# Starting every large on-chip tile at a multiple of 256 bytes in a hybrid decoder block

## The chip, the core and the metric

The kernel runs on one core of a Trainium2 chip. The metric is device time in microseconds (us) of one execution, the median of several runs. The profile is one execution recorded by the hardware profiler; its span runs from the first to the last instruction.

## The reference

The reference is one decoder layer in fp32 over 512 tokens of width 2048. It normalises the tokens, projects them with one large matrix, and splits the columns in two groups: four heads of gated linear attention and four of differential softmax attention. Both outputs go through one output projection and are added to the residual. Then follows a gated MLP with a short causal convolution.

```python
def token_mixer(h, ...):
    proj = h @ w_in                                   # (512, 2048) @ (2048, 6160)
    gq, gk, gv, gg, ga, dq, dk, dv = split(proj)
    o_a = gla_chunked(gq, gk, gv, log_sigmoid(ga @ w_alpha_up + b_alpha) / 16)
    o_a = rmsnorm(o_a, gla_norm) * silu(gg)
    o_b = rmsnorm(diff_attention(dq, dk, dv, lam), diff_norm) * (1 - lambda_init)
    return concatenate([o_a, o_b]) @ w_o              # (512, 2048) @ (2048, 2048)

def conv_ffn(h, ...):
    a, b = split(h @ w_ffn_in)                        # (512, 2048) @ (2048, 2 x 5632)
    a = conv_w[0] * a[t-2] + conv_w[1] * a[t-1] + conv_w[2] * a[t] + conv_b
    return (gelu(a) * b) @ w_ffn_out                  # (512, 5632) @ (5632, 2048)

x = x + rmsnorm(token_mixer(rmsnorm(x, attn_pre_norm)), attn_post_norm)
x = x + rmsnorm(conv_ffn(rmsnorm(x, ffn_pre_norm)), ffn_post_norm)
```

## The kernel before

**Precision.** Large products are made of three fp32r matmuls. Each operand is split into a high part (`act(hi, raw, AF.Copy)` on ScalarE, L110) and the rest (`tt(lo, raw, hi, subtract)` on VectorE, L111). TensorE then adds high x high, high x low and low x high in PSUM. The normalised activations lie in `ah` and `al` (high and low, each `[128, 4, 16, 128]`: partition, block of 128 tokens, block of 128 features, token or feature). The weights come through `raw` or `rt` (as loaded, 4096 bytes per partition) and are split into `whi` and `wlo`, or `xhi` and `xlo` where a fourth buffer is to be had. The small products inside the two kinds of attention, and the transposes against `ident`, are plain fp32.

**Stages, in order of time.** First the head: load the tokens, normalise and transpose them into `ah`/`al`. Then the projections of the mixer, and the output projection:
- `proj_t` and `mm_t` (L146 to L148) stream `ah`/`al` as the moving operand, 512 columns in four pieces of 512 bytes, 8192 bytes apart, against weights from `whi`/`wlo`. The last few stream 256 columns, in two pieces.
- `proj_n` and `mm_n` (L164 to L166) do it the other way round: `whi`/`wlo` move, 2048 contiguous bytes, and a 128-token block of `ah`/`al` is the stationary operand.

The attention heads are generators that run between these projections (`step`, `fill`). Their plain fp32 matmuls include L481 (scores) and L512 (values); L131 is a transpose.

The up-projection of the MLP (827 to 1690 us) uses a Strassen-like scheme with seven products in place of eight. `up_prods` (L893 to L895) streams 256 columns in two pieces of 512 bytes. For four of the seven products they are blocks of `ah`/`al`, with the pieces 8192 bytes apart. For the other three they are sums in tiles of their own, `s5h`, `s5l`, `s2h`, `s2l`, `s3h`, `s3l`, with the pieces 4096 bytes apart. The weights of these products are loaded by SyncE's queue, and partly added to by transfers that GpSimd issues (L842).

The down-projection (1690 to 2105 us) has the same scheme in `down_prods` (L990 to L992), where `whi`/`wlo` or `xhi`/`xlo` move with 512 columns. `last_group` (L1097 to L1099) adds the first columns of the MLP and writes the result.

**Where tiles lie.** Each pool takes its place in the on-chip memory in the order in which the pools are made, from the low end unless `side="right"` is given; every tile is rounded up to 32 bytes per partition. The low 16,384 bytes are not the kernel's, then come four constants of 32 bytes each. Before the change `ident` (512 bytes) and `nhalf` (32) follow, so `ah` begins at 17,056, and everything behind it inherits an odd offset, with small tiles of 32 bytes between. Per partition, in bytes from the start of the memory:

```text
tile             before               after
ah               17056 (160 mod 256)  16640 (0)
al               49824 (160)          49408 (0)
raw              85728 (224)          82176 (0)
whi              102112 (224)         98560 (0)
wlo              114400 (224)         110848 (0)
rt               126688 (224)         123136 (0)
s5h, s2h, s3h    143072, ... (224)    139520, ... (0)
xhi, xlo (MLP)   192352, ... (96)     188672, ... (0)
ident            16512 (128)          225536 (0)
```

All offsets in the column "before" are multiples of 32 and not of 64, except that of `ident`.

Of the kernel before, what the change touches and what calls it, by code (L numbers as in the profile page):

```python
# [9 lines left out]
F32 = mybir.dt.float32  # L10
# [7 lines left out]
P = 128  # L18
D = 2048
S = 512  # L20
NT = S // P
# [6 lines left out]
NF = DFF // P  # L28
# [7 lines left out]
def hybrid_layer(ctx: ExitStack, tc: tile.TileContext, x, attn_pre_norm, w_in, w_alpha_up, b_alpha,  # L36
# [3 lines left out]
    nc = tc.nc  # L40
# [6 lines left out]
    def dma(o, i):  # L47
        return nc.sync.dma_start(out=o, in_=i)
# [7 lines left out]
    mm = nc.tensor.matmul  # L56

    const = ctx.enter_context(tc.tile_pool(name="const", bufs=1))
    small = ctx.enter_context(tc.tile_pool(name="small", bufs=8))
    psm = ctx.enter_context(tc.tile_pool(name="psm", bufs=4, space=PSUM))  # L60
    psa = ctx.enter_context(tc.tile_pool(name="psa", bufs=4, space=PSUM))

    wpool = ctx.enter_context(tc.tile_pool(name="w", bufs=3))

    ident = const.tile([P, P], F32, name="ident")
    make_identity(nc, ident)
    nhalf = const.tile([P, 4], F32, name="nhalf")
    nc.vector.memset(nhalf, -0.5)

    ah = const.tile([P, NT, KT, P], F32R, name="ah")  # L70
    al = const.tile([P, NT, KT, P], F32R, name="al")

    def bank(pool=None):
        return (pool or psa).tile([P, 512], F32, name="bank", tag="bank")
# [21 lines left out]
    def load(src, a):  # L96
        raw = wpool.tile([P, GR], F32, name="raw", tag="raw", bufs=4)
        dma(raw.rearrange("p (a b) -> p a b", a=a), src)
        return raw

    def granule(src, a, raw=None, spare=None, bufs=4):
        if raw is None:
            raw = load(src, a)
        if spare:
            hi = spare.tile([P, GR], F32R, name="xhi", tag="xhi", bufs=bufs)
            lo = spare.tile([P, GR], F32R, name="xlo", tag="xlo", bufs=bufs)
        else:
            hi = wpool.tile([P, GR], F32R, name="whi", tag="whi")
            lo = wpool.tile([P, GR], F32R, name="wlo", tag="wlo")
        act(hi, raw, AF.Copy)  # L110
        tt(lo, raw, hi.bitcast(F32), ALU.subtract)  # L111
        r = "p (a b) -> p a b"
        return hi.rearrange(r, a=a), lo.rearrange(r, a=a)

    def rsqrt_mean(ss, n, width=1):
        t = small.tile([P, width], F32, name="ms", tag="ms")
        nc.gpsimd.tensor_scalar(t, ss, 1.0 / n, EPS, ALU.mult, ALU.add)
        r = small.tile([P, width], F32, name="rs", tag="rs")
        nc.gpsimd.tensor_tensor(r, t, nhalf[:, :width], ALU.pow)
        return r  # L120
# [5 lines left out]
    def transpose_into_act(src, t, slot0, n):  # L126
        for g in range(0, n, 4):
            m = min(4, n - g)
            b = bank()
            for j in range(m):  # L130
                nc.tensor.transpose(b[:, j * P:(j + 1) * P], src[:, (g + j) * P:(g + j + 1) * P], ident)  # L131
            bv = b[:, :m * P].rearrange("p (k c) -> p k c", k=m)
            split(ah[:, t, slot0 + g:slot0 + g + m, :], al[:, t, slot0 + g:slot0 + g + m, :], bv)

    def bcast_row(tile_ap, row):
        dma(tile_ap, row.partition_broadcast(P))
# [23 lines left out]
    def mm_n(banks, t, g, w):  # L160
        for k in range(2):
            s = 2 * g + k
            st, sp = s == 0, s == KT - 1
            mm(banks[t], ah[:, t, s, :], w[0][:, k, :], start=st, stop=False)  # L164
            mm(banks[t], ah[:, t, s, :], w[1][:, k, :], start=False, stop=False)  # L165
            mm(banks[t], al[:, t, s, :], w[0][:, k, :], start=False, stop=sp)  # L166
# [17 lines left out]
    def big8(name):  # L184
        return mx.tile([P, 2048], F32, name=name, tag="big8", bufs=6)
# [8 lines left out]
    def first_half(c):  # L194
        gb = big8("gb")
        jb = mx.tile([P, 1024], F32, name="jb", tag="jb", bufs=1)
        xts = [big8("xt") for _ in range(NT)]
        H2 = [slice(1024 * i, 1024 * (i + 1)) for i in range(2)]
        H4 = [slice(512 * i, 512 * (i + 1)) for i in range(4)]
        rs, raws, w = {}, {}, {}  # L200
        banks = [bank(psm) for _ in range(NT)]
        col = C_GV + 512 * c

        def load_x(t):
            for i in range(2):
                dma(xts[t][:, H2[i]], x2[t * P:(t + 1) * P, H2[i]])

        def load_w(*gs):
            for g in gs:
                raws[g] = load(w_in3[:, 2 * g:2 * g + 2, col:col + 512], 2)  # L210

        def weights(g):
            w[g] = granule(None, 2, raws[g], spare=mx if g == 3 else None, bufs=1)

        def square(t):
            ss = small.tile([P, 2], F32, name="ss2", tag="ss2")
            for i in range(2):
                act(jb, xts[t][:, H2[i]], AF.Square, accum_out=ss[:, i:i + 1])
            sm = small.tile([P, 1], F32, name="ss", tag="ss")
            nc.gpsimd.tensor_tensor(sm, ss[:, 0:1], ss[:, 1:2], ALU.add)  # L220
            rs[t] = rsqrt_mean(sm, D)

        def scale(t, *ps):
            for i in ps:
                stt(xts[t][:, H4[i]], xts[t][:, H4[i]], rs[t], gb[:, H4[i]], ALU.mult, ALU.mult)

        def turn(t, *ps):
            for i in ps:
                transpose_into_act(xts[t][:, H4[i]], t, 4 * i, 4)

        def prods(t, *gs):
            for g in gs:
                mm_n(banks, t, g, w[g])

        load_x(0)
        bcast_row(gb[:, H2[0]], attn_pre_norm[0, H2[0]])
        load_w(0, 1, 2)
        load_x(1)
        load_w(3)
        load_x(2)  # L240
        load_x(3)
        bcast_row(gb[:, H2[1]], attn_pre_norm[0, H2[1]])
        square(0)
        scale(0, 0, 1)
        weights(0)
        turn(0, 0, 1)
        weights(1)
        weights(2)
        square(1)
        prods(0, 0, 1)  # L250
        scale(1, 0, 1)
        prods(0, 2)
        weights(3)
        turn(1, 0, 1)
        square(2)
        prods(0, 3)
        square(3)
        scale(2, 0, 1)
        prods(1, 0, 1, 2)
        turn(2, 0, 1)  # L260
        prods(1, 3)
        scale(3, 0, 1)
        prods(2, 0, 1)
        turn(3, 0, 1)
        scale(0, 2, 3)
        prods(2, 2)
        turn(0, 2, 3)
        scale(1, 2, 3)
        prods(2, 3)
        turn(1, 2, 3)  # L270
        scale(2, 2, 3)
        prods(3, 0, 1)
        turn(2, 2, 3)
        scale(3, 2, 3)
        prods(3, 2)
        turn(3, 2, 3)
        prods(3, 3)
        return banks
# [30 lines left out]
    bcast_row(dnb, diff_norm[0])  # L309
    ts(dnb, dnb, 1.0 - LAMBDA_INIT, None, ALU.mult)  # L310

    lam = const.tile([P, 1], F32, name="lam")
    lt = setup[:, 0:512].rearrange("p (a d) -> p a d", a=4)
    for i, v in enumerate((lambda_q1, lambda_k1, lambda_q2, lambda_k2)):
        bcast_row(lt[:, i, :], v[0])
# [7 lines left out]
    tt(lam, le[:, 0:1], le[:, 1:2], ALU.subtract)  # L323
    ts(lam, lam, LAMBDA_INIT, None, ALU.add)

    cols = const.tile([P, 4 + 4 * NF], F32, name="cols")
    rows = setup[:NF, 1536:2048].rearrange("p (a d) -> p a d", a=4)
    ba = setup[:4, 768:896]
    dma(ba, b_alpha[0].rearrange("(h d) -> h d", d=P))
# [266 lines left out]
    wp = wo.enter_context(tc.tile_pool(name="wo", bufs=1))  # L596
# [2 lines left out]
    g2 = wp.tile([P, D], F32, name="g2")  # L599
    bcast_row(g1, attn_post_norm[0])  # L600
    bcast_row(g2, ffn_pre_norm[0])
    ssm = [wp.tile([P, 4], F32, name=f"ssm{t}") for t in range(NT)]

    def evac_m(c, t, b):
        jk = wp.tile([P, 512], F32, name="jk5", tag="jk5", bufs=1)
# [218 lines left out]
    ff = None  # L824
# [224 lines left out]
    ff = ctx.enter_context(tc.tile_pool(name="ff", bufs=2))  # L1049
    acc = [ff.tile([P, D], F32, name=f"acc{t}", bufs=1) for t in range(NT)]  # L1050
    accp = [ff.tile([P, D // 2], F32, name=f"accp{j}", bufs=1) for j in range(2)]
    ssf = [ff.tile([P, 4], F32, name=f"ssf{t}", bufs=1) for t in range(NT)]
    g3 = ff.tile([P, D], F32, name="g3", bufs=1)
    bcast_row(g3, ffn_post_norm[0])
    downs[0].z0()
# [135 lines left out]
```

## Time and profile before

| | |
|---|---|
| Median of 3 runs | 2177.14 us (2175.53 to 2177.21) |
| The profiled execution's own time | 2177.07 us |
| Its span | 2175.4 us |
| TensorE busy | 2140.5 us (98%) |
| VectorE, ScalarE, GpSimd busy | 65%, 41%, 9% |
| Moved by DMA | 303.83 MB, mean 140 GB/s |
| Head (0 to 54 us) | TensorE busy 41.71 us, DMA 213 GB/s |
| Up-projection (827 to 1690) | TensorE busy 862.61 of 863 us, 7169 matmuls |
| Down-projection (1690 to 2105) | TensorE busy 405.59 of 415 us, 1865 matmuls |

In the profile PE is TensorE's matmuls, PEld its weight loads, DVE VectorE, ACT ScalarE, POOL GpSimd, SP SyncE. A row of a group shows the line, the engine, the tiles as out<-in, the shapes, the count, and then the busy time in us, the mean of one in ns, and the idle time before them with what ended it. A plain fp32 matmul appears as two records. Matmuls overlap in the pipeline, so their durations add up to more than the span. The form column says f32 for fp32 and fp32r alike; the code tells which is which.

### The profile page before, as it was taken

The page shows a single profiled execution, that of the slowest core. Times are in us where ns is not written, and L with a number is a line of the kernel's source. Part 1 is how long each engine was busy: PE and PEld are TensorE (multiplying, and loading weights), DVE is VectorE, ACT ScalarE, POOL GpSimd, SP SyncE. Part 2 cuts the span into 40 slices and gives each one's busy share as a digit, 9 for nine tenths or more (in the row PEclk, how much of TensorE's full clock was granted, in tenths as well). Part 3 has the DMA queues.
Part 4 walks back from the last instruction along what each step waited for, and adds up shares of the span by engine and source line. Part 5 has one row for each costly group of instructions (what it writes and reads, how often), then busy time and mean ns, then how long its engine had stood idle before and what let it go on. Part 6 is the DMA issues. An engine that isn't in the chain of part 4 may idle for free.

```text
span 2175.4 us, 31878 instructions
## 1 busy us (share of the span) xinstructions
PE 2140.5 (98%) x13009; PEld 1893.4 (87%) x13009; DVE 1418.5 (65%) x1721; ACT 901.4 (41%) x1162; POOL 204.8 (9%) x245
## 2 busy tenths in 40 slices
PE   7999999999999999999999999999999899999997
PEld 6778888787888888899999999999999788788886
DVE  5345554443444237688777786777777777888987
ACT  4233332333343224344444544444444464444433
POOL 1000000000000001011111111111011011111101
PEclk9999999999999999999999999999999999999999
DMA  6322222223224335365776757667577677576653
GB/s 212 101 71 78 78 69 78 78 78 84 77 83 167 95 126 184 126 133 129 162 169 152 163 142 181 155 144 183 140 168 181 180 212 211 167 194 174 172 157 136
DMA packets 218472, 303.83 MB, mean 140 GB/s; under 512 B 11777, under 2 KB 155573, under 8 KB 216405
## 3 DMA queue, kind: packets, MB, share of 16 engines
q1 hardware_dynamic: 165204, 238.87, 33.6%
q0 software_dynamic: 53120, 62.92, 18.6%
q8 instruction: 102, 1.67, 0.3%
q14 instruction: 46, 0.37, 0.0%
HBM read 273.97 MB, written 27.79 MB: 139 GB/s over the span
## 4 chain that ended last, share of the span: by engine, by line
PE 50%; issue 43%; POOL 3%; DVE 2%; DMA 1%; ACT 1%; POOLq 0%; SPq 0%; DVEq 0%; ACTq 0%
PE bank L164 7%; PE bank L166 7%; PE bank L165 6%; PE bank L148 5%; PE bank L146 5%; PE bank L147 5%; PE bank L991 3%; PE bank L992 3%; PE bank L990 3%; POOL rt L842 2%; POOL raw L842 2%; PE bank L413 1%; PE bank L481 1%; PE bank L512 1%; PE bank L131 1%
## 5 line engine op out<-in xcount | busy, mean ns | idle before, releaser
L111 DVE TENSOR_TENSOR wlo<-raw,whi 128x1024 fp32r<-128x1024 f32 x307 | 374.4, 1222 | 363.1 <-ACT whi L110 353.0
L110 ACT ACTIVATE whi<-raw 128x1024 fp32r<-128x1024 f32 x307 | 324.8, 1059 | 604.2 <-PE bank L166 160.3
L895 PE MATMUL bank<-ah,wlo 128*128 128x256 f32 x1280 | 353.7, 276 | 0.4 <-DVE wlo L111 0.4
L893 PE MATMUL bank<-ah,whi 128*128 128x256 f32 x1280 | 353.6, 276 | 0.0
L894 PE MATMUL bank<-al,whi 128*128 128x256 f32 x1280 | 353.4, 276 | 0.0
L111 DVE TENSOR_TENSOR wlo<-rt,whi 128x1024 fp32r<-128x1024 f32 x220 | 267.9, 1221 | 94.9 <-ACT whi L110 94.8
L110 ACT ACTIVATE whi<-rt 128x1024 fp32r<-128x1024 f32 x220 | 232.3, 1059 | 229.8 <-PE bank L894 171.5
L895 PEld LDWEIGHTS bank<-ah,wlo 128*128 128x128 f32 x1280 | 240.2, 188 | 0.8 <-DVE wlo L111 0.8
L893 PEld LDWEIGHTS bank<-ah,whi 128*128 128x128 f32 x1280 | 240.4, 188 | 0.1
L894 PEld LDWEIGHTS bank<-al,whi 128*128 128x128 f32 x1280 | 240.3, 188 | 0.1
L164 PE MATMUL bank<-whi,ah 128*128 128x512 f32 x600 | 238.4, 400 | 0.6 <-ACT ah L123 0.6
L165 PE MATMUL bank<-wlo,ah 128*128 128x512 f32 x600 | 236.5, 395 | 0.0
L166 PE MATMUL bank<-whi,al 128*128 128x512 f32 x600 | 236.3, 396 | 0.0
L146 PE MATMUL bank<-ah,whi 128*128 128x512 f32 (+1 forms) x512 | 198.0, 387 | 0.0
L147 PE MATMUL bank<-al,whi 128*128 128x512 f32 (+1 forms) x512 | 196.6, 384 | 0.0
L148 PE MATMUL bank<-ah,wlo 128*128 128x512 f32 (+1 forms) x512 | 196.6, 384 | 0.0
L991 PE MATMUL bank<-wlo,ah 128*128 128x512 f32 x420 | 164.8, 393 | 1.5 <-DVE wlo L111 1.5
L992 PE MATMUL bank<-whi,al 128*128 128x512 f32 x420 | 164.7, 393 | 0.0
L990 PE MATMUL bank<-whi,ah 128*128 128x512 f32 x420 | 156.1, 390 | 0.3 <-DVE acc L998 0.3
L166 PEld LDWEIGHTS bank<-whi,al 128*128 128x128 f32 x600 | 113.1, 189 | 25.6 <-DVE al L124 0.3
L165 PEld LDWEIGHTS bank<-wlo,ah 128*128 128x128 f32 x600 | 113.2, 189 | 24.9 <-DVE wlo L111 0.5
L164 PEld LDWEIGHTS bank<-whi,ah 128*128 128x128 f32 x600 | 113.1, 189 | 24.4 <-ACT ah L123 1.0
(250 smaller groups left out, 4103.9 us busy)
## 6 DMA issues: line engine op xcount, KB each, us to landing
raw<-in_w_in_dram SPq DMA_DIRECT2D x96, 512.0 KB, 3.8
raw<-in_w_ffn_in_dram SPq DMA_DIRECT2D x96, 512.0 KB, 4.7
raw<-in_w_ffn_out_dram SPq DMA_DIRECT2D x48, 512.0 KB, 5.8
rt<-in_w_ffn_in_dram SPq DMA_DIRECT2D x40, 512.0 KB, 6.3
rt<-in_w_ffn_in_dram POOLq DMA_DIRECT2D x40, 512.0 KB, 6.1
raw<-in_w_ffn_in_dram POOLq DMA_DIRECT2D x40, 512.0 KB, 7.0
raw<-in_w_o_dram SPq DMA_DIRECT2D x32, 512.0 KB, 3.8
rt<-in_w_ffn_out_dram SPq DMA_DIRECT2D x20, 512.0 KB, 7.2
```

Source lines behind the costliest of these rows:

```text
L110: act(hi, raw, AF.Copy)
L111: tt(lo, raw, hi.bitcast(F32), ALU.subtract)
L146: mm(o, wh, ah[:, t0:t1, kk, :], start=st, stop=False)
L147: mm(o, wh, al[:, t0:t1, kk, :], start=False, stop=False)
L148: mm(o, wl, ah[:, t0:t1, kk, :], start=False, stop=sp)
L164: mm(banks[t], ah[:, t, s, :], w[0][:, k, :], start=st, stop=False)
L165: mm(banks[t], ah[:, t, s, :], w[1][:, k, :], start=False, stop=False)
L166: mm(banks[t], al[:, t, s, :], w[0][:, k, :], start=False, stop=sp)
L893: mm(o, wh, sh[:, :, kk, :], start=start and kk == 0 and n == 0, stop=False, **NOW)
L894: mm(o, wh, sl[:, :, kk, :], start=False, stop=False, **NOW)
L895: mm(o, wl, sh[:, :, kk, :], start=False, stop=kk == HK - 1, **NOW)
L991: mm(b[j], sh[:, o:o + P], w[1][:, q, :], start=False, stop=False, **NOW)
```

## The change

Four things are done, all to where tiles lie:
- The small tiles (`small`, and a new pool `few` with `ident`, `nhalf`, `lam`, `cols`, `ssm`, `ssf`) go to the other end of the memory with `side="right"`. `ssm` and `ssf` belonged to the pools of their stages.
- A tile `pad` of 128 bytes is put behind the four constants, so that `ah` begins at 16,640 = 65 x 256. It is filled once by VectorE.
- The weight pool is made after `ah` and `al`, behind them as before.
- `ss2` gets four buffers in place of eight; four are used.

Every large tile then begins at a multiple of 256 bytes. The instructions of all engines, their order and what they wait for are the same in both kernels, apart from `pad`'s memset on VectorE. Line numbers behind the first hunk move by 2 to 4 (L111 becomes L115, L893 becomes L897, L990 becomes L994).

```diff
     const = ctx.enter_context(tc.tile_pool(name="const", bufs=1))
-    small = ctx.enter_context(tc.tile_pool(name="small", bufs=8))
+    small = ctx.enter_context(tc.tile_pool(name="small", bufs=8, side="right"))
+    few = ctx.enter_context(tc.tile_pool(name="few", bufs=1, side="right"))
...
-    wpool = ctx.enter_context(tc.tile_pool(name="w", bufs=3))
-    ident = const.tile([P, P], F32, name="ident")
+    ident = few.tile([P, P], F32, name="ident")
     make_identity(nc, ident)
-    nhalf = const.tile([P, 4], F32, name="nhalf")
+    nhalf = few.tile([P, 4], F32, name="nhalf")
     nc.vector.memset(nhalf, -0.5)
+    pad = const.tile([P, 32], F32, name="pad")
+    nc.vector.memset(pad, 0.0)
     ah = const.tile([P, NT, KT, P], F32R, name="ah")
     al = const.tile([P, NT, KT, P], F32R, name="al")
+    wpool = ctx.enter_context(tc.tile_pool(name="w", bufs=3))
...
-            ss = small.tile([P, 2], F32, name="ss2", tag="ss2")
+            ss = small.tile([P, 2], F32, name="ss2", tag="ss2", bufs=4)
...
-    lam = const.tile([P, 1], F32, name="lam")
+    lam = few.tile([P, 1], F32, name="lam")
...
-    cols = const.tile([P, 4 + 4 * NF], F32, name="cols")
+    cols = few.tile([P, 4 + 4 * NF], F32, name="cols")
...
-    ssm = [wp.tile([P, 4], F32, name=f"ssm{t}") for t in range(NT)]
+    ssm = [few.tile([P, 4], F32, name=f"ssm{t}") for t in range(NT)]
...
-    ssf = [ff.tile([P, 4], F32, name=f"ssf{t}", bufs=1) for t in range(NT)]
+    ssf = [few.tile([P, 4], F32, name=f"ssf{t}") for t in range(NT)]
```

## The prediction

> **What bounds the kernel now.** I read the page first: how much of the span TensorE fills, and whether its clock is held back.
>
> ```profile
> span 2175.4 us, 31878 instructions
> ...
> PE 2140.5 (98%) x13009; PEld 1893.4 (87%) x13009; DVE 1418.5 (65%) x1721; ACT 901.4 (41%) x1162; POOL 204.8 (9%) x245
> ...
> PE   7999999999999999999999999999999899999997
> ...
> PEclk9999999999999999999999999999999999999999
> ```
>
> TensorE is busy in 2140.5 of 2175.4 us, at the full granted clock. Only 35 us are idle. The table by stage shows where.
>
> ```profile
> core 0: us, PE busy (x) PEld busy (x) DVE busy (x) ACT busy (x) POOL busy (x), PEclk, DMA share, GB/s
> 0.00:54.00 54.00, 41.71 (x194) 32.72 (x195) 30.48 (x44) 26.37 (x40) 5.60 (x20) 1.00 0.63 213
> ...
> 827.00:1690.00 863.00, 862.61 (x7169) 850.55 (x7168) 651.45 (x667) 400.45 (x444) 105.00 (x88) 1.00 0.65 156
> 1690.00:2105.00 415.00, 405.59 (x1865) 333.62 (x1864) 338.74 (x353) 198.00 (x207) 50.34 (x42) 0.99 0.69 183
> ```
>
> The up-projection (827 to 1690) leaves TensorE no idle time, so there only the pace of the matmuls counts. The head waits 12.3 us, the down-projection 9.4 us. Since the change moves tiles and leaves instructions and waits alone, the next question is whether a matmul's pace depends on where its operands lie. I compared the groups of matmuls by form, which show the mean duration of one.
>
> ```profile
> L895 PE MATMUL bank<-ah,wlo 128*128 128x256 f32 x1280 | 353.7, 276 | 0.4 <-DVE wlo L111 0.4
> L164 PE MATMUL bank<-whi,ah 128*128 128x512 f32 x600 | 238.4, 400 | 0.6 <-ACT ah L123 0.6
> L148 PE MATMUL bank<-ah,wlo 128*128 128x512 f32 x448 | 178.8, 399 | 0.0
> L991 PE MATMUL bank<-wlo,ah 128*128 128x512 f32 x420 | 164.8, 393 | 1.5 <-DVE wlo L111 1.5
> L893 PE MATMUL bank<-s3h,whi 128*128 128x256 f32 x320 | 90.6, 283 | 0.0
> L991 PE MATMUL bank<-xlo,ah 128*128 128x512 f32 x140 | 56.2, 402 | 0.2 <-DVE xlo L111 0.2
> L1097 PE MATMUL bank<-whi,ah 128*128 128x512 f32 x56 | 21.0, 389 | 0.0
> L512 PE MATMUL bank<-dv,aT 128*128 128x256 f32 x80 | 19.9, 379 | 0.0
> L131 PE MATMUL bank<-ident,xr 128*128 128x128 f32 x64 | 7.6, 272 | 0.0
> L481 PE MATMUL bank<-dk,dq 128*128 128x512 f32 x16 | 7.5, 593 | 0.0
> ```
>
> The first tile after the arrow is the moving one. A duration holds the streaming time and a constant pipeline time. The timeline of one engine gives the streaming time by itself, as the distance between starts:
>
> ```profile
> 1299.81 0.28 PE L893 MATMUL bank<-s2h,whi 128*128 128x256 f32 x1
> ...
> 1302.93 0.28 PE L895 MATMUL bank<-s2h,wlo 128*128 128x256 f32 x1
> ```
>
> Between these two rows lie 26 distances: 3.12 us / 26 = 120 ns, so the pipeline part is 283 - 120 = 163 ns. All groups carry it, so a difference of durations is a difference of pace.
>
> Now the yardstick. The plain fp32 groups (L131, L512, L481; not the fp32r of the weight products) step by 593 - 379 = 214 ns for 256 columns and 379 - 272 = 107 ns for 128. They stream one column in 0.836 ns and pay nothing else that depends on form. The fp32r groups stream at about half that per column: 120 ns for 256. At exactly half, an fp32r matmul of 256 columns would last as long as the plain one of 128, that is 272 ns, and one of 512 columns 379 ns. They last longer:
> - 256 columns, moving `ah`/`al`: 276, 4 ns over.
> - 256 columns, moving `s2`, `s3`, `s5`: 283, 11 ns over.
> - 512 columns: 389 to 402, 10 to 23 ns over.
>
> Two pairs differ in the tile alone or nearly so. L893 to L895 with `ah` and with `s3h` have the same shape and weights, and cost 276 and 283. L991 with `wlo` and with `xlo` (both 2048 contiguous bytes) costs 393 and 402. By the placement in the kernel before, `ah` begins 160 bytes past a multiple of 256, the `s` tiles and `whi`/`wlo` 224, and the down-projection's `xhi`/`xlo` 96. So place seems to matter. What isn't in the trace is an fp32r operand that begins at a multiple of 256.
>
> [...]
>
> **The change, part by part.** *Matmul pace.* The counts are 2880 matmuls on `s` tiles (nine groups of 320), 4224 of 256 columns on `ah`/`al` (three groups of 1280, six of 64), and 5136 of 512 columns (L164 to L166 640 each, L146 to L148 448, L990 to L992 560, L1097 to L1099 64). I take 393 for the last, since 399 to 402 hold stalls too.
> 1. The part that differs between tiles: 7 ns x 2880 = 20.2 us, and (393 - 389) x 5136 = 20.5 us. Together 40.7 us. If alignment is the cause, it goes.
> 2. The part common to all fp32r groups: 4 ns x (4224 + 2880) = 28.4 us, and (389 - 379) x 5136 = 51.4 us. Together 79.8 us. All of these operands are unaligned today, so it may go whole, or may belong to fp32r and stay. Its bounds are 0 and 79.8; with no nearer row for either, I take half, 39.9 us.
>
> That makes 80.6 us of TensorE time, between 40.7 and 120.5. In the head, mixer and up-projection it is span, for nothing else is late there (DVE 651 of 863 us).
>
> *Given back in the down-projection.* Its 1680 matmuls of 512 columns hold (4 + 5) x 1680 = 15.1 us of the 80.6. There the weights sometimes arrive late already:
>
> ```profile
> ACT whi L110 <- DMA rt<-in_w_ffn_out_dram: 23.4, 8, 4.8
> ...
> ACT xhi L110 <- DMA raw<-in_w_ffn_out_dram: 18.9, 4, 6.4
> ```
>
> A faster TensorE meets these transfers earlier. I give half back, 7.5 us (bounds 0 and 15.1).
>
> *DMA.* The destination rows in on-chip memory now begin on boundaries.
>
> ```profile
> raw<-in_w_in_dram SPq DMA_DIRECT2D x96, 512.0 KB, 3.8
> raw<-in_w_ffn_in_dram SPq DMA_DIRECT2D x96, 512.0 KB, 4.7
> ```
>
> Both move 512 KB, the second in rows of 1 KB instead of 2 KB, and take 4.7 and 3.8 us: more pieces cost more. Fewer pieces would help only where TensorE waits for DMA, in the head (12.3 us idle) and the down-projection (9.4). I take 2 us gained, with bounds of 0 and 6. [...]
>
> *The rest.* VectorE gets one memset (`pad`, 32 columns), at the start, and a DVE pass of 1024 columns takes 1222 ns:
>
> ```profile
> L111 DVE TENSOR_TENSOR wlo<-raw,whi 128x1024 fp32r<-128x1024 f32 x307 | 374.4, 1222 | 363.1 <-ACT whi L110 353.0
> ...
> L111 DVE TENSOR_TENSOR xlo<-raw,xhi 128x1024 fp32r<-128x1024 f32 x25 | 30.3, 1221 | 18.2 <-ACT xhi L110 18.2
> ```
>
> So the memset is under 1.2 us, on an engine busy 30.5 of the first 54 us: nothing, or 1.2 us if that cover were gone. These rows also show that DVE doesn't care: 1222 ns with tiles at 224 and 1221 with tiles mostly at 96. The small tiles' move, `ss2` with four buffers (four are used) and the earlier allocation of `ssm`/`ssf` add no wait and move no instruction.
>
> *Sum.* The profiled execution took 2177.07 us (span 2175.4 and 1.7 around it), as the median of 2177.14. 2177.07 - 80.6 + 7.5 - 2 = 2102.0 us, which is 3.4% faster. With the bounds: 2177.1 - 120.5 - 6 = 2050.6 at best, and 2177.1 - 40.7 + 15.1 = 2151.5 if only the first part goes and the down-projection keeps all it may.
>
> **The rivals.** *No effect.* The pieces of the `s` tiles lie 4096 bytes apart, those of `ah` 8192, and the change keeps both. If that step makes the 7 ns, the pace stays and only DMA is left: 2175 us, within 0.2% (4.4 us, about what a measurement here can tell from no change). Against it speaks the pair 393/402, which has no such step. [...]
>
> *Slower: moving and weight operands in step.* TensorE reads two streams at once, the moving tile and the next weights. The only pairs that share their offset within 256 bytes today are the `s` tiles and `whi`/`wlo` (both 224), and these are the slow 283; `ah` and `whi` lie 64 apart and cost 276. After the change every pair shares its offset. If that is the cause, `ah` rises to 283: 7 x 4224 = 29.6 us; and 512 columns to twice the excess, 379 + 22 = 401 from 393: 8 x 5136 = 41.1 us. That gives 2177.1 + 70.7 = 2247.8 us, and 2206.7 if only the 256-column groups pay. It decides as soon as the `ah` group reads above 276. Against it: 402 for `xlo` with `ah`, 64 apart, too.
>
> **How the numbers follow.** Forecast family 0.60, for the two pairs that differ by tile and the excess that plain fp32 lacks; no effect 0.10; in step 0.30, since one pair fits it well. Faster, same and slower by over 0.2% are therefore 0.60, 0.10 and 0.30. The forecast's own range is 2050 to 2152. The range for 8 in 10 goes from 2050 to 2222: it holds the forecast, no effect, and a little under half of the slower case, and leaves out about 0.18.
>
> **What would show it.** If the steps are right, the `s` and `ah` groups read the same, near 274, the 512-column ones near 384, plain fp32 stays at 379 and 593, and the up-projection takes 863 - 9 x 2880 - 2 x 3840 ns = 829 us. `s` at 283 with `ah` at 276 means no effect; `ah` at 283 means in step. It would also be wrong if the pace rose and the span didn't, with TensorE idle before L990 on DMA.

## The result: 0.57% slower, and the profile after

The changed kernel takes 2188.9 us (median of 4 runs, 2187.49 to 2190.51) against 2176.74 (4 runs, 2175.53 to 2177.21): 1.0057 times as long, 95% interval 1.004 to 1.0074. The forecast was 2102.0. The profiled execution took 2189.8 us. Its page begins:

```profile
span 2188.1 us, 31879 instructions
...
PE 2152.7 (98%) x13009; PEld 1921.7 (88%) x13009; DVE 1418.9 (65%) x1722; ACT 901.2 (41%) x1162; POOL 204.6 (9%) x245
```

TensorE is busy for 12.2 us more, with as many matmuls, and idle for 35.4 us where it was 34.9. So matmuls have become slower, not waits longer. To see which, I cut both traces at events instead of at times: the first matmul of `up_prods`, the first of the down-projection, the first of `last_group`. (The `mm_t` matmuls with which the MLP begins lie before the first cut.) First the kernel before, then the one after:

```profile
core 0: us, PE busy (x) PEld busy (x) DVE busy (x) ACT busy (x) POOL busy (x), PEclk, DMA share, GB/s
0.00:937.20 937.20, 924.06 (x4417) 760.14 (x4418) 452.92 (x718) 324.74 (x525) 49.64 (x116) 1.00 0.34 105
937.20:1712.70 775.50, 775.50 (x6673) 775.48 (x6672) 589.30 (x596) 368.12 (x401) 101.42 (x80) 1.00 0.67 158
1712.70:2113.10 400.40, 390.99 (x1707) 317.50 (x1706) 329.66 (x344) 190.10 (x197) 46.55 (x39) 0.99 0.70 187
2113.10:2175.40 62.30, 49.99 (x217) 40.29 (x215) 46.60 (x64) 18.46 (x39) 7.21 (x11) 0.93 0.36 135
```

```profile
0.00:927.90 927.90, 914.96 (x4417) 763.14 (x4418) 452.96 (x719) 324.44 (x525) 49.63 (x116) 1.00 0.33 106
927.90:1728.50 800.60, 800.60 (x6673) 800.59 (x6672) 589.94 (x596) 369.22 (x401) 101.44 (x80) 1.00 0.65 153
1728.50:2126.20 397.70, 387.67 (x1706) 317.65 (x1705) 329.33 (x344) 189.07 (x197) 46.40 (x39) 0.99 0.69 188
2126.20:2188.10 61.90, 49.45 (x217) 40.32 (x215) 46.65 (x64) 18.46 (x39) 7.17 (x11) 0.93 0.35 137
```

The stretch of `up_prods` has become 25.1 us longer at the same granted clock of 1.00, with TensorE busy all the time in both. Everything else has become shorter: 9.3 us before it, 2.7 in the down-projection, 0.4 in the last part. The groups of matmuls by form, after, say which matmuls did it (to be read against the rows in the prediction):

```profile
L899 PE MATMUL bank<-ah,wlo 128*128 128x256 f32 x1280 | 362.9, 284 | 0.0
L169 PE MATMUL bank<-wlo,ah 128*128 128x512 f32 x600 | 236.3, 394 | 0.0
L152 PE MATMUL bank<-ah,wlo 128*128 128x512 f32 x448 | 176.8, 395 | 0.0
L995 PE MATMUL bank<-wlo,ah 128*128 128x512 f32 x420 | 164.1, 391 | 2.2 <-DVE wlo L115 2.2
L897 PE MATMUL bank<-s3h,whi 128*128 128x256 f32 x320 | 90.7, 283 | 0.0
L995 PE MATMUL bank<-xlo,ah 128*128 128x512 f32 x140 | 55.9, 399 | 0.6 <-DVE xlo L115 0.4
L516 PE MATMUL bank<-dv,aT 128*128 128x256 f32 x80 | 19.8, 379 | 0.0
L135 PE MATMUL bank<-ident,xr 128*128 128x128 f32 x64 | 7.6, 273 | 0.0
L485 PE MATMUL bank<-dk,dq 128*128 128x512 f32 x16 | 7.5, 593 | 0.0
```

`ah` with 256 columns went from 276 to 284 ns; the `s` tiles stayed at 283; 512 columns went from 399 to 395 (`ah` moving) and from 393 to 391 (`wlo` moving); plain fp32 stayed at 379, 273 and 593. A mean duration holds a pipeline part (163 ns in the prediction's rows) and some stalls (L995 with `xlo`, 399 on average, has a median of 390 and a longest of 795), so I went on to the distance between starts. Four cuts from TensorE's timeline show it, with 256 columns before and after, then with 512 columns before and after (start in us, duration in us, engine, line, tiles):

```profile
1311.92 0.28 PE L895 MATMUL bank<-ah,wlo 128*128 128x256 f32 x1
...
1312.94 0.28 PE L895 MATMUL bank<-ah,wlo 128*128 128x256 f32 x1
```

```profile
1240.02 0.28 PE L897 MATMUL bank<-ah,whi 128*128 128x256 f32 x1
...
1242.90 0.28 PE L897 MATMUL bank<-ah,whi 128*128 128x256 f32 x1
```

```profile
650.20 0.39 PE L166 MATMUL bank<-whi,al 128*128 128x512 f32 x1
...
652.95 0.39 PE L166 MATMUL bank<-whi,al 128*128 128x512 f32 x1
```

```profile
649.91 0.39 PE L168 MATMUL bank<-whi,ah 128*128 128x512 f32 x1
...
652.40 0.39 PE L170 MATMUL bank<-whi,al 128*128 128x512 f32 x1
```

With 256 columns, 9 distances in 1.02 us before (113.3 ns each) and 24 in 2.88 us after (120.0). With 512 columns, 12 in 2.75 us before (229.2) and 11 in 2.49 us after (226.4). The same from all starts of both traces, without the few distances that hold a wait (over 1.15 times the median):

```text
ns from start to start              before   after   matmuls   sum, us
256 columns, ah/al moving            113.6   120.0      4224     +27.0
256 columns, s tiles moving          119.8   120.0      2880      +0.5
512 columns, ah/al moving            233.3   227.8      1344      -7.4
512 columns, whi/wlo/xhi/xlo moving  229.7   227.2      3792      -9.7
```

That is +10.4 us. With the distances that hold a wait counted in, the four groups make +12.6 of the 12.7 us by which the span grew; the waits add most where the weights move.

### The profile page after: what moved, and what is told of

The parts are those of the page before. It is cut to its first block, busy times and chain, and to the rows that moved or that the text cites. A ratio compares the mean times of both kernels' runs of the same rounds, so it can differ in the third digit from the quotient of the medians.

```text
span 2188.1 us, 31879 instructions
## 1 busy us (share of the span) xinstructions
PE 2152.7 (98%) x13009; PEld 1921.7 (88%) x13009; DVE 1418.9 (65%) x1722; ACT 901.2 (41%) x1162; POOL 204.6 (9%) x245
## 3 DMA queue, kind: packets, MB, share of 16 engines
q1 hardware_dynamic: 165204, 238.87, 32.4%
## 4 chain that ended last, share of the span: by engine, by line
issue 50%; PE 42%; POOL 4%; DVE 2%; DMA 1%; ACT 1%; POOLq 0%; SPq 0%; DVEq 0%; ACTq 0%
PE bank L168 7%; PE bank L169 7%; PE bank L170 7%; PE bank L152 5%; PE bank L150 5%; PE bank L151 4%; POOL rt L846 2%; POOL raw L846 2%; PE bank L417 1%; PE bank L995 1%; PE bank L996 1%; PE bank L994 1%; PE bank L485 1%; PE bank L516 1%; PE bank L135 1%
## 5 line engine op out<-in xcount | busy, mean ns | idle before, releaser
L115 DVE TENSOR_TENSOR wlo<-raw,whi 128x1024 fp32r<-128x1024 f32 x307 | 374.7, 1223 | 357.8 <-ACT whi L114 346.7
L899 PE MATMUL bank<-ah,wlo 128*128 128x256 f32 x1280 | 362.9, 284 | 0.0
L898 PE MATMUL bank<-al,whi 128*128 128x256 f32 x1280 | 362.9, 284 | 0.0
L897 PE MATMUL bank<-ah,whi 128*128 128x256 f32 x1280 | 362.9, 284 | 0.0
L115 DVE TENSOR_TENSOR wlo<-rt,whi 128x1024 fp32r<-128x1024 f32 x220 | 268.1, 1222 | 114.9 <-ACT whi L114 114.6
L897 PEld LDWEIGHTS bank<-ah,whi 128*128 128x128 f32 x1280 | 246.3, 192 | 0.1
L898 PEld LDWEIGHTS bank<-al,whi 128*128 128x128 f32 x1280 | 246.2, 192 | 0.1
L899 PEld LDWEIGHTS bank<-ah,wlo 128*128 128x128 f32 x1280 | 246.2, 192 | 0.0
L995 PE MATMUL bank<-wlo,ah 128*128 128x512 f32 x420 | 164.1, 391 | 2.2 <-DVE wlo L115 2.2
L994 PE MATMUL bank<-whi,ah 128*128 128x512 f32 x420 | 156.4, 391 | 0.6 <-DVE acc L1002 0.6
L170 PEld LDWEIGHTS bank<-whi,al 128*128 128x128 f32 x600 | 113.4, 189 | 24.3 <-DVE al L128 0.3
L168 PEld LDWEIGHTS bank<-whi,ah 128*128 128x128 f32 x600 | 113.4, 189 | 24.1 <-ACT ah L127 1.2
L169 PEld LDWEIGHTS bank<-wlo,ah 128*128 128x128 f32 x600 | 113.5, 189 | 23.6 <-DVE wlo L115 0.5
```

Of the source, the lines that this page charges most:

```text
L897: mm(o, wh, sh[:, :, kk, :], start=start and kk == 0 and n == 0, stop=False, **NOW)
L898: mm(o, wh, sl[:, :, kk, :], start=False, stop=False, **NOW)
L899: mm(o, wl, sh[:, :, kk, :], start=False, stop=kk == HK - 1, **NOW)
L995: mm(b[j], sh[:, o:o + P], w[1][:, q, :], start=False, stop=False, **NOW)
```

## The experiments

I call *distance* the offset of the stationary operand's tile less that of the moving one, modulo 256 bytes (pieces and rows within these tiles are multiples of 512 bytes, so the tile's offset is the operand's). In the kernel before it is 64 where `ah` or `al` moves against `whi`/`wlo`, 192 where `whi`/`wlo` move against `ah`/`al`, 64 where the MLP's `xhi`/`xlo` move, and 0 for the `s` tiles; after, it is 0 everywhere. Two tiles are *in step* when their distance is 0. The theory after the result is the prediction's rival "in step", now with the distance deciding and 0 being slow for 256 columns and fast for 512. Its rivals are the absolute place and, for the gain, DMA. Most experiments start from the changed kernel and shift tiles by fillers, each set once by VectorE; to make room the small tiles of the attention and of the row sums get four buffers in place of eight there. The matmuls are the same in all of them, and so is their order, but for a dozen in the last one.

**All tiles 32 bytes on.** If alignment itself mattered, this would undo it; all distances stay 0.

```diff
-    pad = const.tile([P, 32], F32, name="pad")
+    pad = const.tile([P, 40], F32, name="pad")
```

> The changed kernel with every large tile 32 bytes further (pad of 160 bytes in place of 128, and four buffers for five small attention tiles to make room): all tiles still share their offset within 256 bytes, but none is at a multiple of 64. Theory 'in step' (only the offset of the moving tile against the weight tile loaded beside it counts): nothing changes, 284 ns for every 256-column group and 390 for the 512-column ones, 2188 us. Theory 'place of one tile' (a start off a multiple of 64 costs extra lines): at least one of the two groups moves by 3 ns or more.

2188.39 us, with 2176.75 for the kernel before beside it. The groups:

```profile
L899 PE MATMUL bank<-ah,wlo 128*128 128x256 f32 x1280 | 362.5, 283 | 0.3 <-DVE wlo L115 0.3
...
L995 PE MATMUL bank<-wlo,ah 128*128 128x512 f32 x420 | 163.7, 390 | 1.4 <-DVE wlo L115 1.4
...
L897 PE MATMUL bank<-s3h,whi 128*128 128x256 f32 x320 | 90.6, 283 | 0.0
```

No large tile begins at a multiple of 64 bytes any more. From the starts, the four groups take 120.0, 120.0, 227.8 and 227.2 ns (in the order of the table above), as in the changed kernel. The mean durations are within 2 ns, but for `xhi`/`xlo` in the down-projection (2 to 4 ns less; their rows carry waits). Alignment to 64 or 256 bytes has no part in the pace of these matmuls.

**Weight buffers at different distances.** Three kernels place the three buffers of `whi` and of `wlo` 64 bytes apart, modulo 256, while all moving tiles stay. So one trace holds three distances under equal conditions.

```diff
...
+            hi = wpool.tile([P, GR + 16], F32R, name="whi", tag="whi")[:, :GR]
+            if not spacer:
+                spacer.append(wpool.tile([P, 16], F32, name="mid", tag="mid", bufs=1))
+                nc.vector.memset(spacer[0], 0.0)
+            lo = wpool.tile([P, GR + 16], F32R, name="wlo", tag="wlo")[:, :GR]
...
```

The first has the buffers at 0, 64 and 128, the second at 192, 256 and 320 (a filler of 192 bytes behind `al`), the third at 32, 96 and 160 (a filler of 32).

> The changed kernel with buffers of whi and wlo 64 bytes longer, so that their three buffers begin 0, 64 and 128 bytes past a multiple of 256, while ah, al and the s tiles stay at 0. Theory 'in step': the distance between starts goes by the weight buffer: 120 ns (256 columns) beside the buffer at 0, about 113 beside the one at 64 (as ah and whi were 64 apart before), open at 128, and the s tiles pace like ah in each. Theory 'place of the moving tile': ah and s do not move here, so 120 ns beside all three buffers.

> As the run before, but the three weight buffers begin at 192, 256 and 320 past a multiple of 256. 'In step' with a period of 256 bytes: 256 paces like 0 and 320 like 64, and 192 is new. With a period of 512: 256 and 320 are new values. 'Place of the moving tile': 120 ns for all.

> As before with weight buffers at 32, 96 and 160. 'In step': three new values, somewhere from 109 (plain half of fp32) to 120 ns for 256 columns; 96 between the values at 64 and 128. 'Place of the moving tile': 120 ns for all three.

They took 2190.63, 2172.71 and 2206.02 us. From the starts, in ns, with some 1,300 to 1,500 matmuls (256 columns) and 400 to 1,600 (512) behind each number:

```text
                            first kernel         second kernel        third kernel
weight buffer at            0     64    128      192   256   320      32    96    160
256 columns, ah/al moving   119.9 116.8 118.4    113.5 120.0 113.4    118.4 117.9 119.8
512 columns, ah/al moving   228.5 233.3 232.7    229.9 228.4 233.2    233.1 233.9 233.3
512 columns, weights moving 228.8 230.0 232.5    233.2 228.8 230.0    232.9 233.6 233.9
```

Three things follow. The weight tile's place changes the pace of a matmul whose moving tile has not moved (first row). Buffers 256 bytes on behave like buffers at 0 (256 in the second kernel against 0 in the first: 120.0 and 119.9, 228.4 and 228.5, 228.8 both times), so the period is taken as 256 bytes. And for 512 columns the distance orders everything, whichever operand is the weight: a moving weight tile at 64 has distance 192 and takes 230.0, like `ah` against a weight tile at 192 (229.9); a moving weight tile at 192 has distance 64 and takes 233.2, like `ah` against weights at 64 (233.3 and 233.2). Zero is best there (228 to 229); 64, 128 and the odd multiples of 32 are slowest (232 to 234). For 256 columns zero is worst, with 160 as bad (119.8), and 64 or 192 best, but not always by as much: 113.4 at 64 in the second kernel, 116.8 in the first.

**Only the `s` tiles moved, in the kernel before.** This is the test from the other side: it takes away the one pair that was in step.

```diff
+    gap = fp.tile([P, 48], F32, name="gap", bufs=1)
+    nc.vector.memset(gap, 0.0)
```

> The kernel before with one edit: a filler of 192 bytes ahead of the s tiles, so that s5, s2 and s3 begin 160 bytes past a multiple of 256 like ah, 64 away from whi and wlo (224), instead of sharing 224 with them. 'In step': the s groups fall from 283 to about 276 ns, all others stay, and 2880 x 6.5 ns = 19 us go: 2158 us. 'Step between the two pieces' (4096 against 8192 bytes, unchanged here): 283 stays, 2177 us. 'Place of the moving tile alone': 160 paces like ah, also 276; the runs with shifted weight buffers speak on that one.

```profile
L897 PE MATMUL bank<-ah,wlo 128*128 128x256 f32 x1280 | 354.4, 277 | 2.8 <-DVE wlo L111 2.7
...
L895 PE MATMUL bank<-s3h,whi 128*128 128x256 f32 x320 | 88.3, 276 | 0.0
```

The `s` group fell from 283 to 276, as the distance says. The prediction's alignment doesn't give that (the tile went from 224 to 160), nor does the step between the pieces, 4096 bytes as before, by which the rival "no effect" explained the 283. The profiled run took 2164.22 us. But ten runs scatter, four from 2159.75 to 2164.22 and six from 2177.25 to 2184.00, median 2178.05: ratio 0.9988 (0.9962 to 1.0014), no gain. The kernel before does not scatter like that (23 runs beside it, 2174.52 to 2179.15). So the time at distance 64 is not one number.

**High and low weights at different distances.** `whi` at 192, `wlo` at 0, to tell whether a matmul's own weights count or the next one's.

```diff
+    gap = const.tile([P, 48], F32, name="gap")
...
+            if not spacer:
+                spacer.append(wpool.tile([P, 16], F32, name="mid", tag="mid", bufs=1))
...
```

> The changed kernel with whi at 192 and wlo at 0 past a multiple of 256, ah, al and s at 0. It tells which weight tile counts. If it is the one loaded for the next matmul: starts after the first and the third matmul of a triple (the next one uses whi) come 113 ns later, after the second (the next uses wlo) 120. If it is the matmul's own: 113, 113 and 120. If the weight tile did not count: 120 for all. Total about 2188 - 7104 x 4.4 ns = 2157 us if two of three matmuls gain.

2194.25 us, where 2157 was expected. Matmuls with their own weights at 0 (and the next at 192) take 120.8 ns, with their own at 192 and the next at 0 117.3, both at 192 115.3. That leans to a matmul's own weight tile, and so do the few changes of buffer in the second kernel above (own 0, next 192: 120.9; own 64, next 0: 113.7). But none of these reaches 113.4 here, so it doesn't price the rest.

**Distance 0 for 512 columns, 192 for 256.** If both halves of the theory hold, one kernel can have both good paces. `ah` and `al` get room for a second view 64 bytes on, which the up-projection reads, and the `s` tiles lie 64 bytes on; weights stay.

```diff
+    a_tiles = [const.tile([P, N_ACT + 64], F32R, name=n) for n in ("ah", "al")]
...
+    ah, al = view(0, 0), view(1, 0)
+    fh, fl = view(0, 16), view(1, 16)
...
-        up[n] = tuple(v[:, 2 * i:2 * i + 2, HK * j:HK * (j + 1), :] for v in (ah, al))
+        up[n] = tuple(v[:, 2 * i:2 * i + 2, HK * j:HK * (j + 1), :] for v in (fh, fl))
+    gap = fp.tile([P, 16], F32, name="gap", bufs=1)
...
```

> The changed kernel, where the up-projection alone reads ah and al through a view 64 bytes further (each gets 256 bytes more, the transposes ahead of the up-projection write there) and the s tiles lie at 64 too, while whi, wlo and the ah, al of the other stages stay at 0. 'In step': 256-column groups at 113 ns between starts (277 ns), the 512-column ones stay at 227 (390 ns). Against the changed kernel 7104 x 6.6 ns = 47 us go: 2142 us, 1.6% under the kernel before, if nothing is given back. 'Place of the moving tile alone': 64 as a new place, unknown pace.

2174.57 us (12 runs, 2165.61 to 2179.03), ratio 0.9984 (0.9974 to 0.9995): better than after, short of the 2142 that I expected. All 256-column groups run at 117.7 ns, not at 113.4, and 512 columns at 227 to 228.

**The distances of before, at multiples of 64.** One filler of 64 bytes behind `al` in the changed kernel: weights and `s` tiles at 64, `ah` and `al` at 0.

```diff
+    gap = const.tile([P, 16], F32, name="gap")
+    nc.vector.memset(gap, 0.0)
```

> The changed kernel with one part undone: a filler of 64 bytes behind al, so that whi, wlo, xhi, xlo and the s tiles begin 64 bytes past a multiple of 256 and ah, al at 0. That is how far apart they lay in the kernel before, but all at multiples of 64. 'In step': the 256-column groups on ah return to 276 ns (113 between starts), s stays at 283 to 284 (120), the 512-column groups go back to about 393 (230 to 233): 2188.9 - 4224 x 6.5 ns + 16 us = 2177 us. If being a multiple of 64 had a share in the changed kernel's loss or gain, it is not 2177.

```profile
L901 PE MATMUL bank<-ah,wlo 128*128 128x256 f32 x1280 | 353.5, 276 | 0.0
...
L154 PE MATMUL bank<-ah,wlo 128*128 128x512 f32 x448 | 178.9, 399 | 0.0
...
L899 PE MATMUL bank<-s3h,whi 128*128 128x256 f32 x320 | 90.6, 283 | 0.0
```

2175.78 us (11 runs), ratio 0.9996 (0.9987 to 1.0005): the kernel before again, in time and in pace (113.5, 119.8, 233.3 and 229.1 ns from the starts), though the small tiles still lie at the other end. With the first experiment this settles the cause of the loss: it is the distance alone.

**Which distance gives 113, and what keeps it.** Both kernels leave the `s` tiles in step and shift only the view of `ah`/`al`, by 192 bytes (distance 64) or by 64 (distance 192).

The edit is that of the kernel with both paces, without its filler ahead of the `s` tiles, and with these views in the first of the two kernels (the second has 16 in place of 48):

```diff
...
+    fh, fl = view(0, 48), view(1, 48)
...
```

> The changed kernel, where the up-projection alone reads ah and al through a view 192 bytes further, so that whi and wlo lie 64 past them (as in the kernel before), and the s tiles stay in step with the weights at 0. What was seen so far: pairs 64 apart have two paces, 113 and about 118, and came to 113 wherever products in step ran between them. Expected: ah 113 (276 ns), s 120 (283), 512 columns 227 (390): 2188.9 - 4224 x 6.5 ns = 2161 us, 0.7% under the kernel before. If the in-step products between do not set the pace: ah 118, 2180 us.

> As the run before with the view 64 bytes further, so that whi and wlo lie 192 past ah. With weights at 192 beside ah at 0 the pace was 113 where in-step buffers came in between, and 118 where both ah and s lay 192 apart. Expected: the same 2161 us if the in-step s products set it, 2180 us if not.

2167.7 us (5 runs, 2164.45 to 2168.81), ratio 0.9953 (0.994 to 0.9965), and 2184.08 us (6 runs, 2180.77 to 2185.93), ratio 1.0027 (1.0016 to 1.0039). `ah` runs at 113.8 ns at distance 64 and at 117.8 at 192; the `s` tiles at 119.8 or 119.9 and 512 columns at 227 to 229 in both. So these two distances differ, although the second weight experiment had 113.5 at 192.

**All 256-column pairs at 64, and all but `s2`.** Both start from the first kernel of the last experiment. The first puts the `s` tiles 192 bytes on as well. The second does so for `s5` and `s3` and leaves `s2` in step.

```diff
+    gap = fp.tile([P, 48], F32, name="gap", bufs=1)
+    nc.vector.memset(gap, 0.0)
```

```diff
-    for n in ("s5", "s2", "s3"):
+    for n, g in (("s5", 48), ("s2", 16), ("s3", 48)):
+        gap = fp.tile([P, g], F32, name="gap" + n, bufs=1)
+        nc.vector.memset(gap, 0.0)
```

> As the kernel with the view 192 bytes further, and s5, s2 and s3 at 192 too: in the up-projection no product is in step any more, whi and wlo lie 64 past every moving tile, as in the run where only the s tiles were moved. There the executions ran from 2160 to 2184 us. If in-step products are what brings pairs 64 apart to the quick pace: executions scatter again, between 2167.7 - 2880 x 6.5 ns = 2149 us (all at 113) and 2149 + 7104 x 4.4 ns = 2180 us (all at 118). If the pace is set by the distance alone: 2149 us each time.

> As that kernel, but s2 alone stays in step with the weights at 0; s5 and s3 are at 192. So one product of seven is in step, once per unit. If in-step products set the pace: s5 and s3 come to 113 like ah, and 2167.7 - 1920 x 6.5 ns = 2155 us each time, with little scatter. If not: scatter as in the run beside it.

The first took 2166.07 us (6 runs), ratio 0.9943 (0.9921 to 0.9964), and scatters from 2154.38 to 2175.39, as the `s` experiment did. The second took 2159.61 us (5 runs, 2152.22 to 2159.67), ratio 0.9903 (0.9891 to 0.9916). That is the fastest version, 1.0% faster than before and 1.3% faster than after (2159.61 against 2188.9). Its groups, and its up- and down-projection cut at the same events:

```profile
L911 PE MATMUL bank<-ah,wlo 128*128 128x256 f32 x1280 | 353.6, 276 | 1.7 <-DVE wlo L122 1.7
...
L909 PE MATMUL bank<-s2h,whi 128*128 128x256 f32 x320 | 90.4, 283 | 0.0
L909 PE MATMUL bank<-s3h,whi 128*128 128x256 f32 x320 | 88.5, 277 | 0.0
```

```profile
928.80:1693.00 764.20, 763.44 (x6674) 762.95 (x6672) 587.94 (x596) 367.08 (x401) 101.40 (x80) 1.00 0.68 160
1693.00:2096.00 403.00, 388.82 (x1706) 316.67 (x1705) 328.36 (x343) 188.02 (x197) 46.52 (x39) 0.99 0.69 186
```

Against after the up-projection is 36.4 us shorter (800.6 to 764.2), and the down-projection 5.3 longer (397.7 to 403.0): TensorE waits 14.2 us there instead of 10.0.

**Two paces that last.** The up-projection runs in 280 blocks of 24 matmuls that share their weight buffers. Taken by block, the pace at distance 64 is either 113.5 or 117.8 ns, with next to nothing between, and it lasts. With all pairs at 64, the profiled execution has 243 blocks at the first pace and then 37 at the second, to the end. The change falls on a wait of TensorE for weights. Here are two rows before that wait, the row that waited, and two rows behind it:

```profile
1587.96 0.28 PE L911 MATMUL bank<-s5h,wlo 128*128 128x256 f32 x1
...
1590.90 0.28 PE L910 MATMUL bank<-s2l,whi 128*128 128x256 f32 x1
1591.86 0.38 PE L911 MATMUL bank<-s2h,wlo 128*128 128x256 f32 x1 [0.68 <-DVE wlo L122]
1592.09 0.28 PE L909 MATMUL bank<-s2h,whi 128*128 128x256 f32 x1
...
1595.15 0.28 PE L911 MATMUL bank<-s3h,wlo 128*128 128x256 f32 x1
```

There are 26 distances in 2.94 us before (113.1 ns) and 26 in 3.06 us behind (117.7). The other changes between neighbouring blocks at one distance lie at a delayed `wlo` matmul too, 0.17 to 0.44 us from start to start: two where only the `s` tiles were moved (8 blocks at 117.8 between them), one in the kernel with both paces (distance 192; 5 blocks at 113.5, then 275 at 117.8), and one with the view 192 bytes further, where the second pace ended 5 blocks later at products in step. Two more come where other products stand between the blocks. Most waits change nothing: with all pairs at 64, five earlier ones, of 0.3 to 0.6 us from start to start, did not.

So distance 64 keeps the first pace where in-step products come between (all 160 blocks at 64 in the kernel before and in the one with its distances, 153 of 160 with the view 192 bytes further, 238 of 240 with `s2` in step). The first kernel with shifted weight buffers is an exception that I can't explain: 15 of its 93 blocks at 64 have the first pace. Where no 256-column product is in step, executions scatter. All 7104 matmuls of 256 columns at 117.7 instead of 113.5 would be 30 us, which is about the size of the scatter (24.3 and 21.0 us). That the longer executions changed pace earlier is argued, since only one execution of each was profiled; the 37 blocks there cost 37 x 24 x 4.4 ns = 3.9 us.

## Why the prediction was wrong

**The step that failed is the first part of the sum**, "If alignment is the cause, it goes". The two pairs were taken as tiles that differ by their own place. The placements in the text held the other reading, which the prediction put among the rivals: the pairs differ by the distance between the two operands. With all tiles 32 bytes on nothing changes; with the weights and `s` tiles 64 bytes on, and `ah`/`al` where they were, all goes back. So of the 20.2 us for the `s` tiles nothing came (283 before and after), and the `ah` groups took on the same 283 to 284. The other term, (393 - 389) x 5136 = 20.5 us, did not compare places at all: the row with 389 (L1097) has `whi` moving against `ah`, like L164 with 400, the same tiles at the same distance of 192. The pair 393 and 402 did differ in distance, 192 for `wlo` and 64 for `xlo`; from the starts that was 229.3 against 232.7 ns, so about 3 of the 9 ns, and the rest was waits that remained (391 and 399 after, with the starts equal at 227).

**The second part**, half the excess common to all fp32r groups, failed with it. The half was a choice between its bounds, and no run shows any of it as the price of alignment. The groups of 256 columns on `ah`/`al` went up by 6.4 ns instead of down. Those of 512 columns fell, but by 5.5 and 2.5 ns and not by the 9 of the forecast, and for the other reason: at distance 0 they are at their best (227.8 and 227.2 ns). The yardstick itself stands. Half of plain fp32's step would be 107 and 214 ns; in step it is 120 and 227, so 13 ns over at both sizes, as if each matmul paid a price that doesn't depend on its columns. From the starts of before it is 11 and 12: plain fp32 matmuls in a row (transposes against `ident` with 128 columns, `dv` with 256) start 109 and 215 ns apart, as medians.

**The rival "in step"** had the mechanism, and its mark came as written: "`ah` rises to 283" (284). It priced the 256 columns at 7 x 4224 = 29.6 us, and 27.0 were measured. Its other term, 512 columns at twice the excess, was wrong in sign: 401 ns and +41.1 us were expected, 391 to 395 ns and -17.1 us came. This is why even its cheaper end, 2206.7 us, lies above the measured 2189. It had 0.30, and the row that should have raised it stood in the text: 276 and 283 are the same shape and weights, and only distance 0 had the 283. The one counted against it, `xlo` at 402, hardly speaks to it: most of its excess is waits, as said above.

**No effect** as a rival fell too. It put the 7 ns down to the step between the pieces, and the `s` group fell from 283 to 276 ns with that step kept. What held is that the absolute place gives TensorE nothing (all tiles 32 bytes on: 283 ns against 284, 2188.39 us against 2188.9), but the place of two tiles against each other counted. Weights are loaded while matmuls run (before, from 827 to 1690 us, matmuls fill 862.61 and weight loads 850.55 of 863 us), and here a matmul's pace hung on the place of both operands: with the moving tile where it was, a weight buffer 64 bytes on changed it from 119.9 to 116.8 ns.

**DMA.** The forecast was 2 us gained, a term that no run shows. The head's idle time went from 12.3 to 12.1 us, the down-projection's from 9.4 to 10.0, and the packets of the loads' queue did not become fewer (165204 both times). The loads and the busy share of the SyncE queue's packets, first before (the loads are in the prediction), then after:

```profile
q1 hardware_dynamic: 165204, 238.87, 33.6%
```

```profile
q1 hardware_dynamic: 165204, 238.87, 32.4%
...
raw<-in_w_in_dram SPq DMA_DIRECT2D x96, 512.0 KB, 3.7
raw<-in_w_ffn_in_dram SPq DMA_DIRECT2D x96, 512.0 KB, 4.7
```

A load in rows of 1 KB takes 4.7 us as before. Over all kernels this median lies between 4.5 and 5.3 us, and with the loads' tiles at multiples of 256 between 4.5 and 5.0. The share fell from 33.6 to 32.4%, but with all tiles 32 bytes off a boundary it is 32.7%, and with all pairs at 64, where the loads' tiles lie at multiples of 256, it is 33.6% again, so alignment is not shown to have done even that.

**Right.** TensorE sets the time (busy 2152.7 of 2188.1 us), and a difference in pace is span in the up-projection (25.1 us there, for 3840 x 6.4 ns = 24.6 us from `ah`/`al` and 0.5 from the `s` tiles). The give-back in the down-projection exists, though not after this change: idle 9.4 before and 10.0 after. In the fastest version it is 14.2. The memset and the small tiles' move cost nothing that shows: the four groups of matmuls make 12.6 of the 12.7 us. Nor did VectorE's pass change with the place:

```profile
L115 DVE TENSOR_TENSOR wlo<-raw,whi 128x1024 fp32r<-128x1024 f32 x307 | 374.7, 1223 | 357.8 <-ACT whi L114 346.7 <-PE bank L899 6.6 <-PE bank L456 3.6
```

It was 1222 ns.

**What stays open.** Why a wait sometimes changes the pace from 113.5 to 117.8 ns at distances 64 and 192 and mostly doesn't; why a distance of 192 is fast beside other buffers and slow by itself; and what it is in TensorE that makes the distance count. A matmul's own weight tile is what the starts go with (120.8 ns with it at 0 and the next at 192, 117.3 the other way round), and the prediction's "next weights" are not borne out as the tile that counts, but the records tell when a matmul starts and not when its operands are read.

## What to carry to other kernels

When two groups of the same shape differ in pace, list the places of *both* operands before you blame one of them, and change one alone before you move everything: a layout that makes all tiles alike also makes all distances alike. For fp32r matmuls of 256 columns like these, place the stationary tile 64 bytes past the moving one, modulo 256: of the seven distances tried it was the quickest (113.4 ns, though 116.8 and 117.8 were seen too), where the same offset, or 160 bytes, was the slowest (120.0 and 119.8). For 512 columns the same offset was the best one (227 to 229 ns against up to 234), so a shared tile may need a shifted view for each use. Profile more than one execution, or time many, where a gain hangs on a pace of a few nanoseconds.

## What the runs showed of the hardware that I had not expected

- The start-to-start time of an fp32r matmul depends on the distance of its two operands modulo 256 bytes: 113.3 to 120.0 ns for 256 columns, 226.4 to 234 for 512; distance 0 is the slowest for 256 and the quickest for 512. Plain fp32 transposes against `ident`, whose distance became 0 as well, did not change (272 and 273 ns); the plain fp32 rows with 379 and 593 ns had distance 0 both times and say nothing on it.
- Distance 0 gives one steady pace, 120 ns for 256 columns and 227 to 229 for 512, in the changed kernel 13 ns over half of plain fp32's step (107 and 214) at both sizes. Distances 64 and 192 have two paces for 256 columns, 113.5 and 117.8 ns. One lasts for up to 275 blocks and changes at a wait of TensorE; without in-step products between them executions of one program scattered by up to 24 us.
- At the same distance, starting tiles at multiples of 256, 64 or only 32 bytes made no difference to TensorE (284 and 283 ns at distance 0, 276 and 276 at 64), nor did it to VectorE (1223 and 1222) or the loads of 1 KB rows (4.7 us before and after).
